# Sums over channels as products of split operands, and norm 1's row factors transposed later

## The chip, the cores and the metric

The kernel runs on one core of a Trainium2 chip. The core has a matrix engine (TensorE, PE in the profile), a vector engine (DVE), an activation engine (ACT), a general engine (POOL), and DMA queues that SyncE (SP) and POOL issue. Each engine works through its own instructions in order and waits on semaphores for the others. The metric is the time of one execution on the device in microseconds, as a median over runs. Three runs of the kernel before took 1290.13, 1290.21 and 1290.51 us, median 1290.21.

## The reference, cut to what matters

The kernel computes one layer of a sequence model in float32: 1024 tokens, 1024 channels. Two token mixers run on the same normalised input and are merged by gates; then comes a squared-ReLU MLP. There are four RMS norms, each with a mean over the channels of a token.

```python
def rmsnorm(x, gain):
    xf = x.astype(jnp.float32)
    y = xf * lax.rsqrt(jnp.mean(xf * xf, axis=-1, keepdims=True) + RMS_EPS)
    return (y * gain.astype(jnp.float32)).astype(x.dtype)
...
        h = rmsnorm(x, g_pre_mix)                       # norm 1
        proj = jnp.einsum('bsd,de->bse', h, w_in)       # [u_pool | q | k | v]
...
        mix = jnp.einsum('bsd,de->bse', merged, w_out)
        x = x + rmsnorm(mix, g_post_mix)                # norm 2
        h2 = rmsnorm(x, g_pre_mlp)                      # norm 3
        a = jnp.square(jax.nn.relu(jnp.einsum('bsd,df->bsf', h2, w_up)))
        ff = jnp.einsum('bsf,fd->bsd', a, w_down)
        x = x + rmsnorm(ff, g_post_mlp)                 # norm 4
```

The numbers of the norms in the comments are those used below.

## The kernel before

Channels lie on the 128 partitions and tokens along the free axis, in two halves of 512 tokens (h = 0 and 1). A dense layer is a chain of 128x512 products into one PSUM bank. Each operand is split into two parts of the reduced float type fp32r (hi, and lo = value - hi), and mm3 (L104 to L114) makes three products of each step: hi by hi (L112), hi by lo (L113), lo by hi (L114). Weights come by DMA into wraw; ACT casts them to whi (L82), which has three buffers, and DVE makes the remainder wlo (L83).

A norm needs the mean over channels, which lie on partitions. ACT squares the tiles, DVE adds them into acc, and one product with a 128x128 matrix of 1/1024 (ones) leaves the mean ms of every token on all partitions. That product is a plain float32 one. rstd (L145 to L158) then makes the row factor rb: ACT takes a logarithm and an exponential (L153 or L151, and L154), and DVE polishes the result in three steps (L155, L156, L157).

- Norm 1 is in phase_in, in stats(h) (L330 to L340), which is interleaved with the products of the first projection u for the second half (stats_side, L353). Since the gain is already in hT, rb is only applied where a projection leaves PSUM (u_out, L380; job_qk, L464). For v, which has tokens on partitions, rb is needed as a column: four PE transposes (L336) into a tile rt, and a DVE copy of one column of each block into rcol (L337).
- In phase_in the tiles ms and rt of both halves, and the tile dm of pool_mix's first half, share one PSUM buffer (tag "o"). Each has to wait until the one before it has been read.
- u has four groups of channels. Groups 0 to 2 of both halves come first, into banks of two kinds (du and zu); group 3 follows in the loop behind u_out(1), and takes the banks du of group 0 over once DVE's L380 has read them. pool_group and pool_mix make the pooling mixer on DVE, ACT and PE beside it. After the loop come the q and k projections (job_qk, tile dqk), and v (job_v, tile dv, read by L497 with rcol).
- Norms 2 and 3 are in chain(ch, h, mix, acc) (L826, L846), which runs beside other products. Norm 3's result is split by ACT (hi) and DVE (t_lo, L812); with it start the MLP's products, which work on pairs of weights and their sums (L911, L912).
- Norm 4 is norm() inside down() (L1200, L1201). There the last squares are not added to acc: two products, one of acc and one of the last squares, are summed in PSUM. The second half's runs beside the products of p3, and the first half's in two parts of 256 tokens at the end.

The order of the instructions on each engine is not written by hand: a scheduler sets it when the program is built, from the order of the code, the buffers and modelled durations.

Of the kernel before, what the change touches and what calls it, by code (L numbers as in the profile page):

```python
# [19 lines left out]
F32 = mybir.dt.float32  # L20
F32R = mybir.dt.float32r
BF16 = mybir.dt.bfloat16
AF = mybir.ActivationFunctionType
ALU = mybir.AluOpType
# [5 lines left out]
P = 128  # L30
H = 512
# [18 lines left out]
class Block:  # L50
# [106 lines left out]
        nc.vector.scalar_tensor_tensor(out=y, in0=b, scalar=-3.0, in1=y, op0=ALU.add, op1=ALU.mult)  # L157
        return y  # L158

    def split_gain(self, src, gain, r, hi, lo, pool):  # L160

        nc = self.nc
        n = src.shape[-1]
        f = pool.tile([P, H], F32, name="nf", tag="nf", bufs=4)[:, :n]
        nc.vector.scalar_tensor_tensor(out=f, in0=src, scalar=gain, in1=r, op0=ALU.mult, op1=ALU.mult)
        nc.scalar.copy(hi, f)
        nc.vector.tensor_sub(lo, f, hi.bitcast(F32))

    def build(self):
        tc, nc = self.tc, self.nc  # L170
        self.table_inst = None
        order = [(("u", g), O_U + g) for g in (0, 1, 2, 3)]
        order += [(("q", 0), O_QK), (("k", 0), O_QK + 1)]
        self.fill = {
# [10 lines left out]
        }  # L185
        order += [(("v", 0, j), O_V + j) for j in range(2)]
        for h in range(-1, 9):
            for f in self.fill[h]:
                if f[0] == "v":
                    if f[1] == 0:  # L190
                        order += [(("v", 1, j), O_V + 2 + j) for j in range(2)]
                elif f[0] == "g":
                    if f[-1] != 1 or len(f) == 2:
                        order.append((f[:2], O_G + f[1]))
                else:
                    order.append((f, O_QK + 2 * f[1] + (f[0] == "k")))
        order += [(("br", e), O_BR + e) for e in range(8)]
        kept = {3: "t2_hi", 4: "t2_lo"}
        order += [(("out", 0, e), O_OUT + e, (), None, kept.get(e)) for e in range(8)]
        order += [(("out", 1, e), O_OUT + e) for e in (2, 1, 0)]  # L200
        order += [(("up", i), O_UP + self.pair(i)[0]) for i in range(16)]
        self.set_order(order)

        cp = tc.alloc_tile_pool(name="const", bufs=1, side="left")
        self.wp = tc.alloc_tile_pool(name="weights", bufs=1, side="left")
        self.big = tc.alloc_tile_pool(name="big", bufs=1, side="left")
        dp = tc.alloc_tile_pool(name="scratch", bufs=1, space=DRAM)
        self.gscr = [dp.tile([P, 1024], F32, name=f"gscr{i}") for i in range(16)]
        self.yscr = [[dp.tile([P, 1024], F32R, name=f"yscr{i}_{j}") for j in range(2)] for i in range(4)]
        self.pscr = [[dp.tile([P, 4, H], F32, name=f"pscr{i}_{j}") for i in range(4)] for j in range(2)]  # L210
        self.ascr = [[dp.tile([P, 4, H], F32, name=f"ascr{f}_{h}") for h in range(2)] for f in range(8)]
        self.tscr = [dp.tile([P, 4, H], F32, name=f"tscr{f}") for f in range(4)]
        self.wscr = [[dp.tile([P, 4, 512], F32, name=f"wscr{n}_{q}") for q in range(4)] for n in range(4)]
        self.wsums = self.weight_sums()
        self.xscr = [[dp.tile([P, H], F32, name=f"xscr{h}_{e}") for e in range(8)] for h in range(2)]

        self.vt = cp.tile([P, N_VEC], F32, name="vt")
        nc.scalar.preload_act_table_set(TABLES)
        self.ones = cp.tile([P, P], F32, name="ones")
        nc.vector.memset(self.ones, 1.0 / 1024.0)  # L220
        self.one1 = cp.tile([P, 1], F32, name="one1")
        nc.vector.memset(self.one1, 1.0)
        self.eps = cp.tile([P, 1], F32, name="eps")
        nc.vector.memset(self.eps, EPS)
        self.gn = cp.tile([P, 32], F32, name="gn")
        self.eye = cp.tile([P, P], F32, name="eye")

        self.past = cp.tile([P, 1024], mybir.dt.uint8, name="past")
        self.rcnt = cp.tile([P, 16], F32, name="rcnt")

        self.rp = tc.alloc_tile_pool(name="row", bufs=1, side="left")
        self.rb = [self.rp.tile([P, H], F32, name=f"rb{h}") for h in range(2)]
        self.rcol = cp.tile([P, NK], F32, name="rcol")
        edge = tc.alloc_tile_pool(name="edge", bufs=1, side="right")
        self.edge = edge.tile([P, 24], F32, name="edge")
        self.dps = tc.alloc_tile_pool(name="att_d", bufs=2, space=PSUM)
        self.zps = tc.alloc_tile_pool(name="att_z", bufs=1, space=PSUM)
        self.phase_in()
        self.phase_attention()
        self.phase_post()  # L240
        self.phase_mlp()

        edge.release()
        for p in (self.rp, self.big, self.wp, cp, dp):
            p.release()


    def phase_in(self):
        tc, nc = self.tc, self.nc
        pa = tc.alloc_tile_pool(name="in_a", bufs=1, side="right")  # L250
        xs = [pa.tile([P, NK, H], F32, name=f"x{h}") for h in range(2)]

        def load(h, k, n):
            nc.sync.dma_start(xs[h][:, k : k + n, :], self.x[h][:, k : k + n, :])
# [3 lines left out]
        for g in range(3):  # L258
            pool, tag, n = (self.wp, "wraw", 2) if g < 2 else (pa, "uraw", 1)
# [33 lines left out]
        for t, src in zip((self.eye, self.rcnt), self.consts):  # L293
# [4 lines left out]
            out=past, in_=past, pattern=[[1, 1024]], compare_op=ALU.is_ge, fill=0.0, base=P - 1024,  # L298
# [11 lines left out]
        accs = []  # L310
        for h in range(2):
            hi = self.big.tile([P, NK, H], F32R, name=f"hT_hi{h}", tag=f"big_hi{h}")
            lo = self.big.tile([P, NK, H], F32R, name=f"hT_lo{h}", tag=f"big_lo{h}")
            self.hT.append((hi, lo))
            acc = pa.tile([P, H], F32, name="acc", bufs=2)
            accs.append(acc)
            for k in range(NK):
# [3 lines left out]
                    out=lo[:, k, :], in0=xs[h][:, k, :], scalar=g, in1=hi[:, k, :].bitcast(F32),  # L321
# [8 lines left out]
        def stats(h):  # L330
            ms = self.zps.tile([P, H], F32, name="ms", tag="o", bufs=1)
            nc.tensor.matmul(ms, self.ones, accs[h], start=True, stop=True)
            self.rstd(ms, pa, ("sq", 3), out=self.rb[h])
            rt = self.zps.tile([P, H], F32, name="rt", tag="o", bufs=1)
            for j in range(4):
                nc.tensor.transpose(rt[:, j * P : j * P + P], self.rb[h][:, j * P : j * P + P], self.eye)  # L336
            nc.vector.tensor_copy(  # L337
                self.rcol[:, 4 * h : 4 * h + 4].rearrange("p (j o) -> p j o", o=1),
                rt.rearrange("p (j o) -> p j o", o=P)[:, :, 0:1],
            )  # L340
# [35 lines left out]
        def u_out(g, ps):  # L376
            if g not in us:
                us[g] = self.op.tile([P, 1024], F32, name=f"u{g}", tag=f"oT{g}")
            for h, d in ps:
                nc.vector.tensor_mul(us[g][:, h * H : h * H + H], d, self.rb[h])  # L380
# [47 lines left out]
        for h in range(2):  # L428
            d = self.dps.tile([P, H], F32, name="du", tag="d")
            self.dense(d, self.weights(("u", 3)), self.hT[h])  # L430
            u_out(3, [(h, d)])
            if h == 0:
                pool_mix(0, pooled[0])
                pooled.append(pool_group(1))
                u_out(2, list(enumerate(dst[2])))
        self.run(self.job_qk("q", 0, 0))
        pool_mix(1, pooled[1])
        pooled.append(pool_group(2))
# [375 lines left out]
    def chain(self, ch, h, mix, acc):  # L814
# [8 lines left out]
        tmp = self.hp.tile([P, 4, H], F32, name=f"tmp{h}", tag="t3_hi")  # L823
        yield 3
        ms = self.ps.tile([P, H], F32, name="ms", tag="ms", bufs=1)
        nc.tensor.matmul(ms, self.ones, acc, start=True, stop=True)  # L826
        r = self.rstd(ms, ch, None, bufs=1, b=tmp[:, 3, :])
        acc2 = ch.tile([P, H], F32, name="acc2", bufs=1)
        for e in range(8):
# [13 lines left out]
                nc.vector.tensor_add(acc2, acc2, sq)  # L843
        yield 28
        ms = self.ps.tile([P, H], F32, name="ms", tag="ms", bufs=1)
        nc.tensor.matmul(ms, self.ones, acc2, start=True, stop=True)  # L846
        self.rstd(ms, ch, None, out=self.rb[h], b=tmp[:, 3, :])

        def norm(e):
# [192 lines left out]
    def down(self):  # L1042
# [152 lines left out]
        def norm(h, x1, gap, c=slice(0, H), behind=(None,)):  # L1195
# [1 line left out]
            at = gap  # L1197
            yield at
            ms = self.ps.tile([P, H], F32, name="ms", tag="ms", bufs=1)[:, c]
            nc.tensor.matmul(ms, self.ones, accs[h][:, c], start=True, stop=False)  # L1200
            nc.tensor.matmul(ms, self.ones, last[h], start=False, stop=True)  # L1201
            r = self.rb[h][:, c]
            self.rstd(ms, mp, ("r", 4), n=c.stop - c.start, out=r)
            nxt = None if x1 else residual(h, 0)
# [121 lines left out]
```

## Time and profile before

| what | value |
|---|---|
| median of three runs | 1290.21 us |
| profiled execution, its own time | 1291.31 us |
| span in its trace | 1289.5 us |
| mean granted TensorE clock | 0.994 |
| q1, the larger DMA queue, share of 16 engines | 33.8% |
| HBM read and written | 178.10 MB, 83.89 MB |

The page begins with the busy time of each engine, and then shows the span in 40 slices of 32 us; a digit is the busy share of a slice in tenths. PE is the matrix engine, PEld its weight loads, which run beside it. PEclk is the clock that the throttle granted. The kinds of product that take most time are the three of mm3; each group of the page is a line of the code with one form of tiles. Rows in order of time give the start, the duration, the engine, the line, the operation, output and inputs; in brackets stands how long the engine was idle before, and for what it waited. An f32 product is recorded as two matmuls (x2).

### The profile page before, as it was taken

What the parts mean: (1) busy time and instruction counts of PE and PEld (TensorE: products, weight loads), DVE (VectorE), ACT (ScalarE), POOL (GpSimd) and SP (SyncE); (2) the same over time, 40 slices, a digit from 0 to 9 for tenths busy, and PEclk for the clock granted to TensorE, in tenths of its full rate; (3) what the DMA queues carried; (4) which work ended last, traced back from release to release, by engine and by line L of the source; (5) the groups of instructions that cost most, each with busy time, mean ns of one, the idle gap of its engine ahead of it and who ended that gap; (6) DMA issues with size and microseconds to landing.
All of it is one profiled execution on the core that took longest, in us unless ns stands there. A gap on an engine that the chain in (4) does not pass through costs nothing.

```text
span 1289.5 us, 16851 instructions
## 1 busy us (share of the span) xinstructions
PE 1268.3 (98%) x6145; PEld 1063.1 (82%) x6145; DVE 924.2 (72%) x1303; ACT 605.5 (47%) x989; POOL 175.2 (14%) x346
## 2 busy tenths in 40 slices
PE   9899999999999999999999999999999999999996
PEld 6688888998888888888877888888888888888885
DVE  8686587688777756661667979777775655776876
ACT  8145455555555543232446646545554433344341
POOL 1011213202322331000101002211220000001000
PEclk9899999999999999999999999999999999999998
DMA  6152646624837978451338577756569546547641
GB/s 223 50 176 81 225 123 164 131 67 113 214 123 177 296 204 234 158 180 49 136 109 285 184 249 254 244 190 210 190 226 342 186 157 225 190 173 246 239 160 66
DMA packets 75746, 233.72 MB, mean 181 GB/s; under 512 B 8624, under 2 KB 11184, under 8 KB 73488
## 3 DMA queue, kind: packets, MB, share of 16 engines
q1 hardware_dynamic: 47936, 143.64, 33.8%
q0 software_dynamic: 27152, 88.49, 23.1%
q8 instruction: 48, 0.79, 0.3%
q10 hardware_dynamic: 576, 0.52, 0.1%
q14 instruction: 34, 0.28, 0.1%
HBM read 178.10 MB, written 83.89 MB: 203 GB/s over the span
## 4 chain that ended last, share of the span: by engine, by line
PE 88%; DVE 6%; DMA 2%; issue 2%; ACT 1%; SPq 0%; POOL 0%; DVEq 0%; POOLq 0%; ACTq 0%
PE d L114 18%; PE d L112 18%; PE d L113 18%; PE dg L110 5%; PE dg L114 5%; PE dg L113 5%; PE o L606 3%; PE at L581 2%; PE dqk L113 2%; PE dqk L114 2%; PE dqk L110 2%; DMA wraw<-w 2%; PE z L552 1%; PE z L549 1%; DVE wlo L83 1%
## 5 line engine op out<-in xcount | busy, mean ns | idle before, releaser
L113 PE MATMUL d<-blo,whi 128*128 128x512 f32 (+1 forms) x456 | 172.7, 379 | 0.0
L114 PE MATMUL d<-bhi,wlo 128*128 128x512 f32 (+1 forms) x456 | 171.9, 378 | 0.0
L112 PE MATMUL d<-bhi,whi 128*128 128x512 f32 (+1 forms) x456 | 168.4, 378 | 0.0
L562 DVE TENSOR_TENSOR_SCAN F<-F,past 128x384 f32<-128x384 f32 (+3 forms) x96 | 93.5, 974 | 25.8 <-ACT F L553 24.9
L82 ACT CAST whi<-wraw 128x512 fp32r<-128x512 f32 (+1 forms) x88 | 67.7, 799 | 88.5 <-PE d L113 33.9
L110 PE MATMUL dg<-hT_hi,whi 128*128 128x512 f32 x256 | 103.3, 404 | 0.3 <-DVE v L497 0.3
L83 DVE TENSOR_TENSOR wlo<-wraw,whi 128x512 fp32r<-128x512 f32 (+1 forms) x88 | 78.2, 907 | 34.1 <-ACT whi L82 34.1
L113 PE MATMUL dg<-hT_lo,whi 128*128 128x512 f32 x256 | 100.6, 393 | 0.0
L114 PE MATMUL dg<-hT_hi,wlo 128*128 128x512 f32 x256 | 100.4, 392 | 0.0
L113 PEld LDWEIGHTS d<-blo,whi 128*128 128x128 f32 x456 | 85.7, 188 | 16.3 <-issue 0.2
L114 PEld LDWEIGHTS d<-bhi,wlo 128*128 128x128 f32 x456 | 85.8, 188 | 16.0 <-issue 0.2
L112 PEld LDWEIGHTS d<-bhi,whi 128*128 128x128 f32 x456 | 85.5, 188 | 15.9
L553 ACT ACTIVATE F<-z 128x384 f32<-128x384 f32 (+3 forms) x96 | 47.3, 493 | 64.1 <-DVE T L566 38.4
L113 PE MATMUL d<-b_lo,whi 128*128 128x512 f32 x196 | 76.7, 391 | 0.0
L112 PE MATMUL d<-b_hi,whi 128*128 128x512 f32 x196 | 75.6, 390 | 0.0
L114 PE MATMUL d<-b_hi,wlo 128*128 128x512 f32 x196 | 75.3, 392 | 0.1
L1093 DVE TENSOR_TENSOR wlo<-slots_hi,whi 128x1024 fp32r<-128x1024 f32 x29 | 35.5, 1224 | 52.6 <-ACT whi L1091 52.5
L1091 ACT CAST whi<-slots_hi 128x1024 fp32r<-128x1024 f32 x29 | 30.5, 1051 | 84.5 <-PE d L113 64.9
L589 DVE TENSOR_TENSOR alo<-at,ahi 128x512 fp32r<-128x512 f32 (+1 forms) x80 | 50.6, 633 | 26.6 <-ACT ahi L588 25.9
L1091 ACT CAST whi<-slots_lo 128x1024 fp32r<-128x1024 f32 x27 | 28.4, 1052 | 72.9 <-PE d L113 59.2
L566 DVE TENSOR_TENSOR T<-T,F 128x127 f32<-128x127 f32 (+4 forms) x96 | 53.1, 556 | 10.2 <-POOL T L556 4.2
L1093 DVE TENSOR_TENSOR wlo<-slots_lo,whi 128x1024 fp32r<-128x1024 f32 x27 | 33.0, 1222 | 36.7 <-ACT whi L1091 36.7
(305 smaller groups left out, 3335.2 us busy)
## 6 DMA issues: line engine op xcount, KB each, us to landing
wraw<-w SPq DMA_DIRECT2D x80, 512.0 KB, 4.3
wscr<-w POOLq DMA_DIRECT2D x24, 1024.0 KB, 9.4
ext_b<-ascr SPq DMA_DIRECT2D x40, 512.0 KB, 4.4
gscr<-gs POOLq DMA_DIRECT2D x32, 256.0 KB, 4.6
gate<-gscr POOLq DMA_DIRECT2D x16, 512.0 KB, 3.7
pscr<-p SPq DMA_DIRECT2D x32, 256.0 KB, 3.7
braw<-w SPq DMA_DIRECT2D x16, 512.0 KB, 5.4
ascr<-c POOLq DMA_DIRECT2D x32, 256.0 KB, 5.2
```

The source lines that it names most:

```text
L82: nc.scalar.copy(hi[:, c], raw[:, c])
L83: self.last_lo = nc.vector.tensor_sub(lo[:, c], raw[:, c], hi[:, c].bitcast(F32)).ins
L110: nc.tensor.matmul(ps, wh, rh, start=first and i == 0, stop=False)
L112: nc.tensor.matmul(ps, wh, rh, start=first and i == 0, stop=False)
L113: nc.tensor.matmul(ps, wh, rl, start=False, stop=False)
L114: nc.tensor.matmul(ps, wl, rh, start=False, stop=last and i == n - 1)
L553: nc.scalar.activation(f[:, c : c + n], z[:, :n], AF.Sigmoid, scale=-1.0)
L562: nc.vector.tensor_tensor_scan(fr, fr, past[:, c : c + n][:, ::-1], 1.0 if top else f[:, c + n : c + n + 1], ALU.mult, ALU.max)
L566: nc.vector.tensor_mul(tl[:, c:e], tl[:, c:e], f[:, c + 1 : e + 1])
L589: nc.vector.tensor_sub(lo[:, c0:], at[:, c0:], hi[:, c0:].bitcast(F32))
L1091: last_split[0] = nc.scalar.copy(hi, src).ins
L1093: last_split[1] = nc.vector.tensor_sub(lo, src, hi.bitcast(F32)).ins
```

## The change

The diff, cut to its core:

```diff
-    def split_gain(self, src, gain, r, hi, lo, pool):
...
+    def channel_sum(self, ps, acc, pool, tag, bufs):
+
+        nc = self.nc
+        hi, lo = (pool.tile([P, H], F32R, name=f"acc_{n}", tag=tag, bufs=bufs) for n in ("hi", "lo"))
+        nc.scalar.copy(hi, acc)
+        nc.vector.tensor_sub(lo, acc, hi.bitcast(F32))
+        nc.tensor.matmul(ps, self.ones_r, hi, start=True, stop=False)
+        nc.tensor.matmul(ps, self.ones_r, lo, start=False, stop=True)
...
-        self.ones = cp.tile([P, P], F32, name="ones")
-        nc.vector.memset(self.ones, 1.0 / 1024.0)
-        self.one1 = cp.tile([P, 1], F32, name="one1")
-        nc.vector.memset(self.one1, 1.0)
+        self.ones_r = cp.tile([P, P], F32R, name="ones")
+        self.ones = self.ones_r.bitcast(F32)
...
+        mean = pa.tile([P, P], F32, name="mean")
+        nc.vector.memset(mean, 1.0 / 1024.0)
+        nc.vector.tensor_copy(self.ones_r, mean)
...
             ms = self.zps.tile([P, H], F32, name="ms", tag="o", bufs=1)
             nc.tensor.matmul(ms, self.ones, accs[h], start=True, stop=True)
             self.rstd(ms, pa, ("sq", 3), out=self.rb[h])
+
+        def columns(h):
+
             rt = self.zps.tile([P, H], F32, name="rt", tag="o", bufs=1)
             for j in range(4):
                 nc.tensor.transpose(rt[:, j * P : j * P + P], self.rb[h][:, j * P : j * P + P], self.eye)
...
                 u_out(2, list(enumerate(dst[2])))
+        for h in range(2):
+            columns(h)
         self.run(self.job_qk("q", 0, 0))
...
-        nc.tensor.matmul(ms, self.ones, acc, start=True, stop=True)
+        if h == 0:
+            nc.tensor.matmul(ms, self.ones, acc, start=True, stop=True)
+        else:
+            self.channel_sum(ms, acc, ch, "nf", 2)
...
-        nc.tensor.matmul(ms, self.ones, acc2, start=True, stop=True)
+        if h == 0:
+            nc.tensor.matmul(ms, self.ones, acc2, start=True, stop=True)
+        else:
+            self.channel_sum(ms, acc2, ch, "nf", 2)
...
-            nc.tensor.matmul(ms, self.ones, accs[h][:, c], start=True, stop=False)
-            nc.tensor.matmul(ms, self.ones, last[h], start=False, stop=True)
+            if h == 0:
+                nc.tensor.matmul(ms, self.ones, accs[h][:, c], start=True, stop=False)
+                nc.tensor.matmul(ms, self.ones, last[h], start=False, stop=True)
+            else:
+                nc.vector.tensor_add(accs[h], accs[h], last[h])
+                self.channel_sum(ms, accs[h], mp, "r", 4)
```

There are two parts. For the second half of the tokens, norms 2, 3 and 4 sum over channels with two fp32r products, of the hi and the lo part of the sum of squares, in place of one f32 product (two in norm 4, where a DVE addition now joins the last squares to the sum first). ACT and DVE make the two parts. The matrix of means becomes an fp32r tile, filled by a memset and a DVE copy. Norm 1, and all norms of the first half, keep their f32 products. The second part moves the transposes of norm 1 out of stats(h): those of both halves now stand behind the loop over u's last group, ahead of the q projections. split_gain and one1 had no use.

The scheduler's order changes with it. On PE, towards the end of the first three groups of u, before (-) and now (+); zu is a bank of the projection, and the number 290 or 291 marks the second half's operand:

```order
 L112 MATMUL zu<-hT_hi_290,whi 128x512
 L113 MATMUL zu<-hT_lo_291,whi 128x512
-L114 MATMUL zu<-hT_hi_290,wlo 128x512
-L112 MATMUL zu<-hT_hi_290,whi 128x512
-L113 MATMUL zu<-hT_lo_291,whi 128x512
-L114 MATMUL zu<-hT_hi_290,wlo 128x512
-L112 MATMUL zu<-hT_hi_290,whi 128x512
-L113 MATMUL zu<-hT_lo_291,whi 128x512
-L336 MATMUL rt<-eye,rb_165 128x128 x4
+L333 MATMUL ms<-acc,ones 128x512
```

The transposes of the first half (rt) stood here, and the second half's sum (ms, now L333) stands six products ahead of their place. Before, that sum came 20 products after the transposes. A few us later on PE, where group 3 of u begins (du, operand 249):

```order
 L112 MATMUL zu<-hT_hi_290,whi 128x512
-L332 MATMUL ms<-acc,ones 128x512
 L113 MATMUL zu<-hT_lo_291,whi 128x512
 L114 MATMUL zu<-hT_hi_290,wlo 128x512
-L336 MATMUL rt<-eye,rb_166 128x128 x4
+L112 MATMUL zu<-hT_hi_290,whi 128x512
+L113 MATMUL zu<-hT_lo_291,whi 128x512
+L114 MATMUL zu<-hT_hi_290,wlo 128x512
+L112 MATMUL zu<-hT_hi_290,whi 128x512
+L113 MATMUL zu<-hT_lo_291,whi 128x512
+L114 MATMUL zu<-hT_hi_290,wlo 128x512
 L112 MATMUL du<-hT_hi_249,whi 128x512
```

Before, the second sum, two products and the second transposes came directly ahead of du; now only products do, and 28 of them stand between the second sum and du. The two moved sets of transposes now stand among the products of the q projection: the first of them 25 products after the last product of pool_mix(0), the second 29 products later. On ACT the cast of the weights for q's projection now stands between the logarithm and the exponential of norm 1's second half; the cast that stood there before is the next one.

On DVE and ACT, norm 3 of the second half changes as well. DVE before, from the last squares added to the start of the normalised tiles (mix):

```order
L843 TENSOR_TENSOR acc_6277<-acc_6277,tmp_6246 128x512 x6
L83 TENSOR_TENSOR wlo<-wraw,whi 128x1024 x2
L155 SCALAR_TENSOR_TENSOR tmp_6246<-ms,rb_166 128x512
L156 TENSOR_TENSOR tmp_6246<-tmp_6246,rb_166 128x512
L83 TENSOR_TENSOR wlo<-wraw,whi 128x1024
L157 SCALAR_TENSOR_TENSOR rb_166<-tmp_6246,rb_166 128x512
L851 SCALAR_TENSOR_TENSOR mix_0_5908<-mix_0_5908,gn,rb_166 128x512
```

And DVE in the changed kernel at the same place:

```order
L852 TENSOR_TENSOR acc_6282<-acc_6282,tmp_6246 128x512 x6
L83 TENSOR_TENSOR wlo<-wraw,whi 128x1024
L165 TENSOR_TENSOR acc_lo<-acc_6282,acc_hi 128x512
L83 TENSOR_TENSOR wlo<-wraw,whi 128x1024 x2
L155 SCALAR_TENSOR_TENSOR tmp_6246<-ms,rb_163 128x512
L156 TENSOR_TENSOR tmp_6246<-tmp_6246,rb_163 128x512
L157 SCALAR_TENSOR_TENSOR rb_163<-tmp_6246,rb_163 128x512
L863 SCALAR_TENSOR_TENSOR mix_0_5908<-mix_0_5908,gn,rb_163 128x512
```

The new subtraction (L165) stands between the weight splits, and all three splits now come ahead of the norm's own three steps, where one of them came after the second step before. On ACT the logarithm was followed directly by the exponential; now a weight cast and the copy of a finished product (p) stand between the two. Further on, before the MLP's first products, four subtractions t_lo followed the last weight split (L83); now five do, since one that stood ahead of it comes behind it. In norm 4 of the second half the sum's product of hi comes 24 products later than the f32 sums did, and that of lo nine or ten after it. Elsewhere the order on PE is nearly the same.

More of the change, by code (lines that the diff above doesn't have):

```diff
@@ L158, in rstd @@
         return y
-    def split_gain(self, src, gain, r, hi, lo, pool):
+    def channel_sum(self, ps, acc, pool, tag, bufs):
         nc = self.nc
[L163 to L167, printed above, removed]
+        hi, lo = (pool.tile([P, H], F32R, name=f"acc_{n}", tag=tag, bufs=bufs) for n in ("hi", "lo"))
[3 more added lines that the diff above has]
+        nc.tensor.matmul(ps, self.ones_r, lo, start=False, stop=True)
     def build(self):
```

## The prediction

> **What bounds the kernel now.** I read the shares of busy time first, then what TensorE (PE) waited for, then the one long wait in order of time, and last the granted clock around it.
>
> ```profile
> span 1289.5 us, 16851 instructions
> PE 1268.3 (98%) x6145; PEld 1063.1 (82%) x6145; DVE 924.2 (72%) x1303; ACT 605.5 (47%) x989; POOL 175.2 (14%) x346
> PEclk9899999999999999999999999999999999999998
> ...
> PE rt L336 <- DVE rb L157: 4.6, 1, 4.6
> PE dv L112 <- DVE v L497: 0.4, 1, 0.4
> PE dg L110 <- DVE v L497: 0.3, 1, 0.3
> ```
>
> PE is busy for 98% of the span. What can be saved is therefore PE work, PE waits, or clock. One wait stands out in the list of waits (total, times, longest, in us): the transposes of norm 1's second row factor waited 4.6 us for DVE. The clock row dips once after the start, in the second slice (32 to 64 us), which is where this wait lies. The rows around it, in order of time (start, duration, engine, what waited for what):
>
> ```profile
> 41.40 1.02 PE L332 MATMUL ms<-acc,ones 128*128 128x512 f32 x2
> 41.86 0.80 PE L113 MATMUL zu<-hT_lo,whi 128*128 128x512 f32 x1
> 42.46 0.69 ACT L153 ACTIVATE rb<-ms,eps 128x512 f32<-128x512 f32 x1 [5.52 <-PE ms L332]
> 42.50 0.40 PE L114 MATMUL zu<-hT_hi,wlo 128*128 128x512 f32 x1
> 43.05 1.03 ACT L82 CAST whi<-wraw 128x1024 fp32r<-128x1024 f32 x1
> 46.70 0.69 DVE L157 SCALAR_TENSOR_TENSOR rb<-nb,rb 128x512 f32<-128x512 f32 x1
> 47.31 1.28 DVE L380 TENSOR_TENSOR u<-du,rb 128x512 f32<-128x512 f32 x2
> 47.45 1.11 PE L336 MATMUL rt<-eye,rb 128*128 128x128 f32 x4 [4.55 <-DVE rb L157]
> 48.21 0.77 PE L112 MATMUL du<-hT_hi,whi 128*128 128x512 f32 x1
> ...
> 61.30 0.39 PE L112 MATMUL dqk<-hT_hi,whi 128*128 128x512 f32 x1
> ```
>
> PE runs the sum over channels (ms), two more products, and then stands from 42.90 to 47.45 while ACT and DVE turn ms into rb. The clock falls in this wait:
>
> ```profile
> 41.00:48.00 7.00, 2.45 (x10) 1.44 (x9) 3.82 (x6) 2.15 (x3) 0.00 (x0) 0.84 0.25 71
> 48.00:53.00 5.00, 5.00 (x15) 3.98 (x14) 5.00 (x10) 0.00 (x0) 0.00 (x0) 0.54 0.06 23
> 53.00:61.00 8.00, 8.00 (x37) 6.59 (x36) 7.21 (x13) 1.05 (x1) 0.00 (x0) 1.00 0.01 2
> 966.00:1190.00 224.00, 224.00 (x990) 185.54 (x989) 141.82 (x138) 91.76 (x99) 6.40 (x12) 1.00 0.62 216
> ```
>
> The columns are stretch, length, busy time and count of PE, weight loads, DVE, ACT and POOL, then the clock. A mean of 0.84 over 7 us is 2.2 us at half clock, so it fell at about 45.8, and 0.54 over the next 5 us puts its return at about 52.6. The last row gives the price of one 128x512 product at full clock: 224.00 / 990 = 0.226 us. (The matmul durations of single rows overlap, so starts are what I subtract.)
>
> **The change, part by part.** The profiled execution took 1291.31 us, 1.10 above the median of 1290.21. I sum against the former and carry the result to the latter.
>
> *1. The second ms comes earlier.* The order of PE's instructions now has ms (second half) where the first half's transposes stood, less six products; 28 products follow it and then du. In the old order it had to wait its turn for the one PSUM buffer that ms and rt share.
>
> ```profile
> 30.37 0.68 DVE L328 TENSOR_TENSOR acc<-acc,sq 128x512 f32<-128x512 f32 x1
> 35.90 1.05 ACT L82 CAST whi<-wraw 128x1024 fp32r<-128x1024 f32 x1 [3.70 <-PE zu L113]
> 36.38 0.60 PE L336 MATMUL rt<-eye,rb 128*128 128x128 f32 x4
> 36.73 0.48 PE L114 MATMUL zu<-hT_hi,wlo 128*128 128x512 f32 x1
> ```
>
> The old first transposes started at 36.38; six products earlier is 36.38 - 6 x 0.226 = 35.02. The sum's input acc is complete at 31.05, so nothing holds it there. An f32 sum costs 42.50 - 41.40 - 0.23 = 0.87 us. With 28 products behind it, PE reaches du at 35.02 + 0.87 + 28 x 0.226 = 42.22 instead of 48.21: **-5.99 us**. This counts the idle time and both sets of transposes as gone from here.
>
> Is the wait then gone, or does du inherit it? The same DVE chain that releases rt also frees du's PSUM bank: du needs the first of the two L380 multiplies, which ended at about 47.95, 0.26 before du started. So moving the transposes alone would gain next to nothing; the earlier ms is what pays. On ACT a weight cast stands between the two steps of the norm, at 35.90 before, released by PE. It comes 0.87 later now, behind ms: 36.77. From such a cast to the end of the first L380 the old chain took 47.95 - 43.05 = 4.90. That frees the bank at 41.7, and PE arrives at 42.22. The margin is 0.5 us. If one more cast of 1.05 stood ahead, du would wait 0.5; zero is my value, 0.5 the bad end.
>
> *2. The clock stays up.* From 48.21 to 61.30 PE ran 48 products of du in 13.09 us. At 0.226 they take 10.85: **-2.24 us**. Without a PE wait of several us there is no row in this stretch that would lower the clock. If it fell nonetheless, 0.
>
> On the timed runs, as against the profiled one, a page speaks against counting this. The Trainium skill ("TensorE: Matmul & The Clock Gate", section "What's actually happening") says that the clock halves after at least one idle window of about 3.4 us, and that the window is free-running. An estimate from that page: a wait of 4.55 us holds a whole window in (4.55 - 3.4) / 3.4 = 1/3 of the phases only, so the median run would not have lost the clock and could not regain it. The trace shows a fall after 2.9 us of idle time, which that window as stated would not give.
>
> *3. The transposes are paid later.* Four cost 36.73 - 36.38 = 0.35 us at full clock, and two sets now stand between the q projections: **+0.70**. The end to the bad side is 48.21 - 47.45 = 0.76 a set at half clock, +1.52.
>
> *4. What follows, up to the attention.* PE arrives 8.23 - 0.70 = 7.5 us earlier there. DVE's own chain starts from the first L380, which moves by 47.95 - 41.7 = 6.2. If DVE were the limit, PE would give back 7.5 - 6.2 = 1.3. If PE stays the limit, and v's multiply (L497) is in time, the two waits of 0.4 and 0.3 go. I take **-0.4**, near the latter, since DVE follows PE through much of this stretch (it sat 3.40 us before the row at 66.99 below). Ends: -0.7 and +1.3.
>
> *5. Norms 2 and 3, second half.* Each f32 sum of 0.87 becomes two products of 0.45: -0.42 each. The new ACT copy and DVE subtraction stand ahead of the sum. In norm 2 DVE has 6.06 us of idle time soon after, which hides them:
>
> ```profile
> 677.05 1.23 DVE L83 TENSOR_TENSOR wlo<-wraw,whi 128x1024 fp32r<-128x1024 f32 x1 [6.06 <-ACT whi L82]
> ...
> 705.02 0.63 ACT L154 ACTIVATE rb<-rb 128x512 f32<-128x512 f32 x1
> 706.90 1.05 ACT L82 CAST whi<-wraw 128x1024 fp32r<-128x1024 f32 x1 [1.25 <-DMA wraw<-w]
> 707.85 0.58 ACT L959 COPY p<-d 128x512 f32<-128x512 f32 x1
> 709.12 0.69 DVE L157 SCALAR_TENSOR_TENSOR rb<-tmp,rb 128x512 f32<-128x512 f32 x1
> 740.09 2.51 DVE L812 TENSOR_TENSOR t_lo<-mix,t_hi 128x512 fp32r<-128x512 f32 x4
> 750.11 0.40 PE L113 MATMUL d<-b_lo,whi 128*128 128x512 f32 x1
> 750.57 0.50 PE L114 MATMUL d<-t_hi,wlo 128*128 128x512 f32 x1
> ```
>
> Norm 3 is less lucky. In the new order the norm's second ACT step (the exponential, at 705.02 before) stands behind the cast at 706.90 and the copy at 707.85, and DVE's three steps behind one more weight split. The exponential then ends at 708.43 + 0.63 = 709.06, and three DVE steps of 0.69 with small gaps end at about 711.25 instead of 709.81: 1.45 late. DVE then works through the normalised tiles up to 742.6 and makes the first pair's weight remainders, for which PE already waits 0.23 (750.11 to 750.57 is 0.46): no slack. One more t_lo subtraction (at 740.09, four take 2.51, or 0.6 each) now comes behind the last weight split instead of ahead of it, which takes 0.6 of the lateness off the path. So 1.45 - 0.6 = 0.85 is late there, norm 3's own 0.42 is lost in that wait, and norm 2's is kept: 0.85 - 0.42 = **+0.43**. Ends: -0.84 if nothing is late, 1.45 + 0.58 (one more copy ahead) - 0.42 = +1.6.
>
> *6. Norm 4, second half.*
>
> ```profile
> 1196.83 1.02 PE L1200 MATMUL ms<-acc,ones 128*128 128x512 f32 x2
> 1197.68 1.02 PE L1201 MATMUL ms<-sq,ones 128*128 128x512 f32 x2
> 1198.77 0.40 PE L114 MATMUL d<-bhi,wlo 128*128 128x512 f32 x1
> ```
>
> Two f32 sums with one product among them take 1198.77 - 1196.83 = 1.94, so 1.71 without it. Two split products take 0.45: **-1.26**. The extra DVE addition of 0.69 and the split are hidden by later work: 80 us of products follow, and DVE is busy only 141.82 of 224 us here.
>
> *7. Start.* One DVE cast in place of a memset, before the first product is possible: 0.
>
> Sum: -5.99 - 2.24 + 0.70 - 0.40 + 0.43 - 1.26 = -8.76. 1291.31 - 8.76 = 1282.55, and 1.10 less on the median: **1281.5 us**.
>
> **The rivals.**
>
> *DVE becomes the limit (0.16).* The bad ends above at once or in part: +1.7 at the attention, +1.2 at the pair, +0.5 at du, +0.8 for slow transposes. For it speaks that DVE is the engine waited for in every row of the list above; against it the slack before 66.99. Time: 1283.4 to 1285.8.
>
> *The clock gives nothing back on the median (0.08).* Either du still waits long enough, or the timed runs had full clock. The sum is short by term 2: 1281.5 + 2.24 = 1283.7. The three timed runs of before lie within 0.38 us, less than 2.24, so all of them had the fall or none had. The free-running window of the Trainium skill's clock page would give this time; that the runs agree so closely speaks against its chance phase.
>
> *The wait moves from rt to du (0.09).* If the bank of du came free only at its old 47.95, terms 1, 2 and 4 shrink to 0.26 in all: 1290.21 - 0.26 + 0.70 + 0.43 - 1.26 = 1289.8. That is the case in which the change does not do what its order promises. For it: du hangs on the same chain. Against: every step of that chain is released by ms or by a cast that PE releases early.
>
> *The wait comes back at the moved transposes, and the kernel is slower (0.06).* The first moved set needs the shared buffer, which pool_mix(0) holds until its L419 has read dm:
>
> ```profile
> 66.29 0.39 PE L114 MATMUL dm<-ph,wml 128*128 128x512 f32 x1
> 66.99 1.41 DVE L419 SCALAR_TENSOR_TENSOR u<-dm,vt,win 128x512 fp32r<-128x512 f32 x2 [3.40 <-ACT win L418]
> ```
>
> Before, L419 ended 68.40 - 66.68 = 1.7 us after the last dm product. In the new order 25 products (5.7 us) stand between, so PE has 4.0 us in hand; the weight split (1.23) and q steps (3 x 0.69) now ahead of L419 on DVE could take 3.3 of it. If DVE were later than that by W, PE would stand for W and, from about 3 us on, lose the clock's 2.24 again. The gain is used up at W = 8.76 - 2.24 = 6.5 us. At W = 10 it is 1281.5 + 10 + 2.24 = 1293.7. For it: PE comes 8 us earlier to work that DVE has only 6 us earlier. Against: 6.5 us more is far beyond any DVE queue seen here.
>
> **How the numbers follow.** The forecast (1279.6 to 1283.4, with the good ends of terms 4 and 5: -0.3 and -1.27) gets 0.58, something better 0.03, the rivals 0.16, 0.08, 0.09 and 0.06 in the order above. The range 1279.6 to 1285.8 holds forecast and the first two rivals, 0.82. A measurement here can tell about 0.2% (2.6 us) from no change, so faster means under 1287.6: 0.58 + 0.03 + 0.16 + 0.08 = 0.85. Within: 0.09. Slower: 0.06.
>
> **What would show it.** Right: no PE wait before du, granted clock 1.00 between 41 and 61 us, du starting near 42.2, split sums that take about 0.45, a wait of about 1 us at the first pair's remainder near 742 (750 less 8). Wrong: an idle PE before du, rt or dv; a clock below 1 before 70 us; or a wait at the first pair longer than 2.5 us. If the clock row dips in both kernels, term 2 was no gain.

## The result and the profile after

The changed kernel takes 1296.35 us (six runs, 1296.05 to 1296.80), the kernel before 1290.36 (six runs, 1289.94 to 1292.05): a ratio of 1.0045, with a 95% interval of 1.0032 to 1.0058. It is slower by 6 us, where 1281.5 was forecast and 1285.8 was the upper end of the range. The profiled execution has a span of 1294.5 us. Among the comparisons below, one of the four executions of e3 took 3300.68 us and is left out of its ratio; the only trace kept of e3 is of that execution, with every fp32r product of 128x512 at about 619 ns for a reason that is not known, so e3 is read by its times alone.

From the page of the changed kernel, the span, the busy shares, the clock row and the shares of the chain that ended last; then its list of PE's waits (total, times, longest):

```profile
span 1294.5 us, 16855 instructions
PE 1278.2 (99%) x6143; PEld 1060.0 (82%) x6143; DVE 927.5 (72%) x1307; ACT 609.5 (47%) x992; POOL 175.4 (14%) x346
PEclk9999999999999999999999999999999999999998
PE 98%; DVE 1%; DMA 0%; ACT 0%; SPq 0%; issue 0%; DVEq 0%
...
PE idle L308 <- DVE zero L305: 1.4, 1, 1.4
PE d L112 <- DVE oT L619: 0.9, 1, 0.9
PE ms L1213 <- DVE acc L1253: 0.8, 1, 0.8
```

All that the forecast wanted to see at norm 1 is there: the wait of rt has gone, those of dv and dg too, and the clock row has no dip. Yet PE is busy for 1278.2 us instead of 1268.3, with two recorded matmuls fewer. So the time did not go into a wait. PE does the same work for longer, at full clock. The same stretches as before (length, busy time and count of PE, weight loads, DVE, ACT, POOL, then clock, DMA share, GB/s) show where:

```profile
41.00:48.00 7.00, 7.00 (x33) 5.79 (x32) 7.00 (x12) 1.06 (x1) 0.00 (x0) 1.00 0.11 43
48.00:53.00 5.00, 5.00 (x24) 4.14 (x23) 5.00 (x9) 1.19 (x2) 0.00 (x0) 1.00 0.28 107
966.00:1190.00 224.00, 224.00 (x962) 180.03 (x962) 136.12 (x131) 86.42 (x91) 5.67 (x12) 1.00 0.60 208
```

In the last stretch PE is busy throughout and the clock is 1.00 in both kernels, but it does 962 products in 224 us where it did 990: 0.233 us each instead of 0.226. PE's own rows of the changed kernel in order of time show the step from one to the other inside the MLP:

```profile
801.16 0.39 PE L114 MATMUL d<-t_hi,slo 128*128 128x512 f32 x1
801.39 0.39 PE L112 MATMUL d<-t_hi,shi 128*128 128x512 f32 x1
801.62 0.39 PE L113 MATMUL d<-t_lo,shi 128*128 128x512 f32 x1
801.84 0.40 PE L114 MATMUL d<-t_hi,slo 128*128 128x512 f32 x1
802.08 0.39 PE L112 MATMUL d<-t_hi,whi 128*128 128x512 f32 x1
802.31 0.40 PE L113 MATMUL d<-t_lo,whi 128*128 128x512 f32 x1
802.55 0.39 PE L114 MATMUL d<-t_hi,wlo 128*128 128x512 f32 x1
```

The moving operand (t_hi, t_lo, the two parts of norm 3's result) comes from the same side of memory throughout. While the weights are shi and slo (the two parts of a sum of weights), starts lie 0.22 to 0.23 apart; from the product ahead of the first whi on, 0.23 to 0.24. What sets shi apart from whi is where the tiles lie. Start addresses in bytes per partition, as the built programs list them:

```
tile                   side    before   after
one1                   left     17248   (gone)
eps                    left     17280    17248
whi, first buffer      left     27264    27232
hT_hi, b_hi of h = 0   left     51840    51808
shi, first buffer      right   155520   155520
```

The diff also deletes one1, a tile of 4 bytes that nothing read. Tiles are placed in steps of 32 bytes (one1 and eps, of 4 bytes each, lie 32 apart), so everything behind it on the left side moved down by 32. Tiles on the right side stayed. Before, every operand of an fp32r product started at the same remainder modulo 256 (27264, 51840 and 155520 all leave 128). Afterwards left tiles leave 96 and right tiles 128. The 128x512 products of the changed kernel's trace, sorted by the remainders of their moving operand and of the next product's weights, which load beside it:

```
moving  next weights  products  median spacing (ns)
  96        96          2117         227
  96       128           365         235
 128        96          2048         234
 128       128           256         230
(kernel before: all 4778 at 128 and 128, median 227)
```

Equal remainders keep 227 ns. (In the last group 181 products lie in the MLP, with a median of 227; 59 lie in the attention, at 230. The attention's products with k as moving operand had 230 before the change too.) Unequal ones cost 234 or 235. This is theory A of the experiments, first held with a unit of 64 bytes: a product is slower where its moving operand and the weights differ in phase, that is, in the remainder of their start addresses. Rival B is that the change's work slows the products, rival C that a tile at certain addresses is slow by itself. 2413 pairs at 233.3 - 226.7 = 6.6 ns (the means in stretches of the MLP) are 15.9 us, close to the 14.9 by which the forecast was missed.

### The profile page after: what moved, and what is told of

Same layout as the page of the kernel before. It is cut to its first block, busy times and chain, and to the rows that moved or that the text cites. A ratio compares the mean times of both kernels' runs of the same rounds, so it can differ in the third digit from the quotient of the medians.

```text
span 1294.5 us, 16855 instructions
## 1 busy us (share of the span) xinstructions
PE 1278.2 (99%) x6143; PEld 1060.0 (82%) x6143; DVE 927.5 (72%) x1307; ACT 609.5 (47%) x992; POOL 175.4 (14%) x346
## 4 chain that ended last, share of the span: by engine, by line
PE 98%; DVE 1%; DMA 0%; ACT 0%; SPq 0%; issue 0%; DVEq 0%
PE d L113 20%; PE d L114 20%; PE d L112 20%; PE dg L114 5%; PE dg L110 5%; PE dg L113 5%; PE o L612 3%; PE at L587 2%; PE dqk L114 2%; PE dqk L113 2%; PE dqk L110 2%; PE z L558 1%; PE z L555 1%; PE dv L114 1%; PE dv L113 1%; PE dv L112 1%
## 5 line engine op out<-in xcount | busy, mean ns | idle before, releaser
L83 DVE TENSOR_TENSOR wlo<-wraw,whi 128x512 fp32r<-128x512 f32 (+1 forms) x88 | 78.2, 907 | 30.8 <-ACT whi L82 30.8
```

The source lines that it names most:

```text
L83: self.last_lo = nc.vector.tensor_sub(lo[:, c], raw[:, c], hi[:, c].bitcast(F32)).ins
```

## The experiments

**One: the address alone (e1 to e4).** Each runs the same instructions in the same order on every engine as the kernel it starts from; only places differ.

e1, the changed kernel with 32 bytes put back:

```diff
-        self.eps = cp.tile([P, 1], F32, name="eps")
+        self.eps = cp.tile([P, 9], F32, name="eps")[:, :1]
```

> The changed kernel with 32 bytes per partition put back ahead of all other tiles of the left side of SBUF (a wider eps tile; nothing reads the new columns). Every engine runs the same instructions in the same order. Theory A (a product is 6.5 ns slower where the start addresses of its moving operand and of the next product's weights differ by 32 bytes modulo 64; 2413 of the changed kernel's 128x512 products do, and none did before): the 15.7 us are gone, 1281 to 1283 us, pitch 227 ns throughout the MLP. Rival B (the new splits, sums or the moved transposes slow the products): unchanged, 1296. Rival C (a tile that is off a multiple of 64 is slow by itself): as A, 1281 to 1283.

Measured: 1280.56 us, ratio to before 0.9924 (0.9910 to 0.9939). The changed kernel is 15.8 us faster for a slot of 32 bytes that nobody reads, and it is now faster than both kernels.

e2, the kernel before with its left side moved down:

```diff
-        self.one1 = cp.tile([P, 1], F32, name="one1")
-        nc.vector.memset(self.one1, 1.0)
-        self.eps = cp.tile([P, 1], F32, name="eps")
+        pair = cp.tile([P, 2], F32, name="one1")
+        nc.vector.memset(pair[:, :1], 1.0)
+        self.eps = pair[:, 1:2]
```

> The kernel before with one1 and eps in one tile, so that the left side moves down by 32 bytes as in the changed kernel; the same instructions in the same order. Theory A: 2404 products at 6.5 ns more are 15.6 us, so 1304 to 1306 us, with the 4.6 us wait of rt still there and a pitch of 233 ns in most of the MLP. Rival B: 1290, as before. Rival C: as A, 1304 to 1306.

Measured: 1306.52 us, ratio 1.0125 (1.0110 to 1.0140): 16.1 us more. The shift costs the same with nothing else of the change present, so rival B is out. The stretch 966 to 1190 us, first of e1 and then of e2:

```profile
966.00:1190.00 224.00, 224.00 (x990) 185.49 (x989) 145.67 (x143) 91.39 (x98) 4.27 (x8) 1.00 0.62 216
```

```profile
966.00:1190.00 224.00, 224.00 (x963) 180.10 (x962) 135.20 (x131) 88.83 (x95) 4.83 (x9) 1.00 0.58 203
```

990 products against 963 in the same time: e1 has the spacing of the kernel before, e2 that of the changed one.

e3, the changed kernel with the right side moved down as well:

```diff
-        self.edge = edge.tile([P, 24], F32, name="edge")
+        self.edge = edge.tile([P, 32], F32, name="edge")[:, :24]
```

> The changed kernel, its left side where the change puts it (32 modulo 64), with the right side moved by 32 bytes as well (a wider edge tile). All operands of products then start at 32 modulo 64, but none differs from its neighbour. Same instructions, same order. Theory A: 1281 to 1283 us, pitch 227. Rival B: 1296. Rival C (each tile off a multiple of 64 is slow): all 4700 products pay, some 1311 us.

Measured: 1280.26 us, ratio 0.9922 (0.9905 to 0.9938). No operand starts at a multiple of 64 here, and the loss is gone all the same. Rival C is out: it is the difference between the two operands that counts.

e4, the changed kernel with its left side moved up by 64:

```diff
-        self.eps = cp.tile([P, 1], F32, name="eps")
+        self.eps = cp.tile([P, 17], F32, name="eps")[:, :1]
```

> The changed kernel with the left side moved by 64 bytes from where the change puts it, so that it is at 32 modulo 64 again, one slot higher than before the change. Same instructions, same order. Theory A: the phase is again apart by 32, so 1296 us as the changed kernel. Were it the place as such, or one conflict of two certain tiles, rather than the phase modulo 64: another time, near 1282. Rival B: 1296.

Measured: 1296.87 us, ratio 1.0052 (1.0035 to 1.0068). Another place with the same difference, and the same loss.

**Two: the period (e8, e9, e10).** e8 puts the left side of the changed kernel 64 bytes above its place in the kernel before:

```diff
-        self.eps = cp.tile([P, 1], F32, name="eps")
+        self.eps = cp.tile([P, 25], F32, name="eps")[:, :1]
```

> The changed kernel with the left side 64 bytes above its place in the kernel before. Phase modulo 64 as there, modulo 128 not. Theory A with 64 bytes as the unit: as e1_left_back_by_32, 1280 to 1281 us. If the unit is 128 bytes: 1296, as the changed kernel, or more.

Measured: 1296.34 us, ratio 1.0049 (1.0035 to 1.0063). My unit of 64 bytes was wrong: a difference of 64 costs as much as 32. e9, the same with 128 bytes:

```diff
-        self.eps = cp.tile([P, 1], F32, name="eps")
+        self.eps = cp.tile([P, 41], F32, name="eps")[:, :1]
```

> The changed kernel with the left side 128 bytes above its place in the kernel before; same instructions, same order. In the kernel before, operands whose phases differ by 256 bytes run at 227 ns, and e8_left_up_64 showed 64 to be as slow as 32. Theory A with a period of 128 bytes: as e1_left_back_by_32, 1280 to 1281 us. With a period of 256 bytes: 1296.

Measured: 1296.21 us, ratio 1.0040 (1.0026 to 1.0055). So 128 isn't the period either. In the kernel before, 365 pairs of remainder 128 and 384 modulo 512 keep a median of 227, so 256 is the first period that fits.

e10 measures the cost by itself. Its core (a moving operand shifted by m bytes, weights by w, over eight PSUM banks):

```diff
+        def stretch(steps):
+            nonlocal n
+            for i in range(64):
+                m, w = steps[i % len(steps)]
+                a, c = 64 + m // 4 + 512 * (i % 2), 64 + w // 4 + 128 * (i % 8)
+                nc.tensor.matmul(banks[n % 8], wt[:, c : c + P], mov[:, a : a + H], start=True, stop=True)
+                n += 1
```

> A kernel of 24 stretches of 64 fp32r products of 128x512, with no other engine at work; it computes nothing of the layer, and only the spacing of its products is read. Stretches 1 to 14 move the start of the moving operand by 0, 0, 4, 8, 16, 32, 48, 64, 96, 128, 160, 192, 224 and 256 bytes against fixed weights; 15 to 19 move the weights by 4, 16, 32, 64, 128; 20 moves both by 32; 21 to 24 alternate between two phases, so that the moving operand agrees with its own weights (21, 23) or with the next product's weights (22, 24). Theory A: 227 ns at 0 and 256, about 233 at 32, 64, 96, whichever operand moves; 227 where both move; and where they alternate, 233 if own and next weights both count, 227 in 21 and 23 if the own weights decide, 227 in 22 and 24 if the next do. At 4, 8 and 16 bytes open: 227 if the unit is 32 bytes, 233 if any shift counts. Rival (the slower spacing needs the traffic of the other engines): 227 everywhere.

Two groups of its page, all of PE's work and one of the two casts that are all of DVE's:

```profile
L74 PE MATMUL bank<-mov,wt 128*128 128x512 f32 x1536 | 358.0, 395 | 7.8 <-DVE mov L65 7.8
...
L65 DVE CAST mov<-raw 128x2048 fp32r<-128x2048 f32 x1 | 1.2, 1219 | 0.0
```

Mean of 54 spacings in the middle of each stretch, in ns, from the starts in the trace (the first of the two stretches at 0, whose first products lie about 0.4 us apart, is left out):

```
moving by   0     4     8     16    32    48    64    96    128   160   192   224   256
          226.7 236.7 231.6 231.7 233.4 233.3 228.9 233.3 233.3 234.3 233.3 233.3 226.7
weights by        4           16    32          64          128
                232.4       233.3 233.3       233.3       232.5
both by 32                                                226.7
alternating, own weights agree and the next differ by 32  233.3
alternating, next weights agree and own differ by 32      231.6
alternating by 64, own agree / next agree                 231.6 / 231.7
```

The traffic of other engines isn't needed. Every difference tried that isn't a multiple of 256 bytes costs 2 to 10 ns in 227, a shift by one element too. It costs whichever operand moves, though not the same: moving by 4 is the dearest at 236.7, weights by 4 have 232.4. Where the phases alternate, both orders are slow: a product's moving operand has to agree with its own weights and with the next ones. The trace of the changed kernel says the same: 147 of its products agree with their own weights and not with the next, at a median of 235, and 20 the other way round, at 233.

**Three: the parts of the change, on the old layout (e5, e6, e7).** e5 is the kernel before with the transposes split off from stats(h) and called after the loop, as in the change; one1 stays.

```diff
             self.rstd(ms, pa, ("sq", 3), out=self.rb[h])
+        def columns(h):
             rt = self.zps.tile([P, H], F32, name="rt", tag="o", bufs=1)
...
+        for h in range(2):
+            columns(h)
         self.run(self.job_qk("q", 0, 0))
```

> The kernel before with the transposes moved and nothing else (sums stay f32; one1 stays, so all tiles stay where they were). By terms 1 to 4 of the prediction: -5.99 - 2.24 + 0.70 - 0.40 = -7.9, so 1282 to 1283 us, no wait of PE before du, full clock from 41 to 61 us. Rival (du inherits the wait): 1289 to 1290, with a PE wait before du that ends with L380.

Measured: 1282.67 us, ratio 0.9944 (0.9931 to 0.9956): -7.6 us against 1290.29. There is no wait before du. In its trace du starts at:

```profile
42.00 0.39 PE L112 MATMUL du<-hT_hi,whi 128*128 128x512 f32 x1
```

42.22 was worked out. e6 is e1 with the transposes put back into stats(h), so that only the split sums are new.

```diff
-        def columns(h):
...
-        for h in range(2):
-            columns(h)
```

> The split sums of norms 2, 3 and 4 with norm 1's transposes left in stats(h), and the left side of SBUF where it was before the change. By terms 5 and 6: +0.43 - 1.26 = -0.8, so 1289 to 1290 us, with the 4.6 us wait of rt still there and a small wait at the first pair of the MLP. If the products' lower cost counted in full (-0.84 - 1.26): 1288.3. If the added work on ACT and DVE cost more than the products save: over 1290.5.

Measured: 1288.25 us, ratio 0.9985 (0.9976 to 0.9994): -2.0 us, more than the -0.8 expected and at the good end of term 5; its interval, -3.1 to -0.8, just reaches the expected value.

e7 is e1 with norm 3's second half back on its f32 product.

```diff
-            self.channel_sum(ms, acc2, ch, "nf", 2)
+            nc.tensor.matmul(ms, self.ones, acc2, start=True, stop=True)
```

> The changed kernel with the left side put back by 32 bytes, and norm 3 of the second half with its f32 product again. By term 5 the split of norm 3 cost 0.85 of lateness and saved 0.42 that was lost in the wait: 0.4 us less than e1_left_back_by_32, so 1280.1 us, and no wait of d L113 for b_lo at the first pair. Rival (the split was free there): 0.4 us more than that kernel, 1281.0.

Measured: 1284.31 us, ratio 0.9949 (0.9937 to 0.9962), 3.75 us slower than e1. It doesn't isolate norm 3. With that edit the scheduler also put the work of the first MLP pairs in another order on DVE, ACT and SP. PE's waits in it:

```profile
PE d L114 <- DVE slo L924: 1.1, 2, 0.9
...
PE d L112 <- DVE u L1012: 0.6, 1, 0.6
PE d L113 <- DVE b_lo L818: 0.4, 1, 0.4
```

The wait for b_lo, which I had put down to norm 3's lateness, stays at 0.4 us: it lies at 656 us, ahead of norm 2's sum and 39 us before norm 3's. 0.7 more at slo and 0.6 at u are new. The f32 sum accounts for another 0.4. The remaining 2 us are not explained; 0.7 of them lie, in the profiled executions, ahead of that wait (655.83 us against 655.09 in e1).

## Why the prediction was wrong

**The step that failed** is term 7, "One DVE cast in place of a memset, before the first product is possible: 0", together with what I put into it. The diff's deletions, one1 among them, I counted as instructions only. That the deleted tile moves every left tile by 32 bytes had no term at all, and no rival covered it: all of mine were waits or the clock. It cost 15.8 us (after to e1; 16.1 from before to e2), more than the whole gain. The other side of the same fault is the price of "one 128x512 product at full clock: 224.00 / 990 = 0.226 us", which I carried to the new kernel as if it were a constant. It holds only while the operands' phases agree.

The rest can be read off e1, e5 and e6, where the layout is as before:

- *Terms 1 to 4* (-7.93 in all): right in sum. e5 gave -7.6. In the changed kernel's trace, the rows of the steps that were worked out:

```profile
34.76 1.02 PE L333 MATMUL ms<-acc,ones 128*128 128x512 f32 x2
36.52 1.05 ACT L82 CAST whi<-wraw 128x1024 fp32r<-128x1024 f32 x1
40.80 1.28 DVE L384 TENSOR_TENSOR u<-du,rb 128x512 f32<-128x512 f32 x2
42.01 0.39 PE L112 MATMUL du<-hT_hi,whi 128*128 128x512 f32 x1
67.25 0.60 PE L340 MATMUL rt<-eye,rb 128*128 128x128 f32 x4
```

ms starts at 34.76 (35.02 worked out), the cast at 36.52 (36.77), the first L384 ends at about 41.4 (41.7), du starts at 42.01 (42.22). All of these are about 0.25 early because PE is: the same product starts at 14.58 us instead of 14.84. The margin before du is the half microsecond that was stated. The moved transposes have no wait in the list, and the waits of dv and dg are gone.

- *Term 2* depends on the execution. e2 has the same wait for rt, but its clock in the two stretches reads:

```profile
41.00:48.00 7.00, 2.45 (x11) 1.49 (x9) 4.09 (x6) 2.15 (x3) 0.00 (x0) 0.93 0.27 74
48.00:53.00 5.00, 5.00 (x19) 4.04 (x18) 5.00 (x10) 0.00 (x0) 0.00 (x0) 0.75 0.01 3
```

That is 1.0 and 2.5 us at half clock, 3.5 together, against 2.2 and 4.6 (6.8) in the profiled execution of before. So the wait cost less clock there. Half-clock stretches of 3.5 and 6.8 us, one and two steps of about 3.4 us, agree with the free-running window in the Trainium skill ("TensorE: Matmul & The Clock Gate", "What's actually happening"); and the three executions profiled with this wait (before, e2, e6) all lost some clock. e5's -7.6 lies nearer to the sum with this term (-7.9) than to that without (-5.7), but its interval (-8.9 to -5.7) reaches to both. The granted clocks on record speak for the term: the fifteen executions of before in that comparison have a mean of 0.9945, e5's five one of 0.9966. Over some 1289 us that is 2.7 us of full clock, where the term took 2.24.

- *Term 5* (+0.43): wrong sign by the rows of e1, small. Norm 3 and the first pair there:

```profile
694.70 0.39 PE L166 MATMUL ms<-acc_hi,ones 128*128 128x512 f32 x1
696.86 1.04 ACT L82 CAST whi<-wraw 128x1024 fp32r<-128x1024 f32 x1
700.52 0.69 DVE L157 SCALAR_TENSOR_TENSOR rb<-tmp,rb 128x512 f32<-128x512 f32 x1
735.30 0.69 DVE L932 TENSOR_TENSOR sums<-wraw 128x512 f32<-128x512 f32 x1 [1.31 <-DMA wraw<-w]
740.95 0.47 PE L114 MATMUL d<-t_hi,wlo 128*128 128x512 f32 x1
741.26 0.40 PE L112 MATMUL d<-t_hi,whi 128*128 128x512 f32 x1
```

I had the cast wait for its weights as late as before. Here it follows the logarithm at once, 2.16 us after the sum began instead of 3.66, and L157 ends 6.51 us after the sum's start instead of 6.57. Nothing was late: DVE still waits 1.31 us for weights ahead of the pair, and PE's spacing there is 0.31, so it waits 0.08. The step that failed here is "no slack": in the kernel before, DVE already waited for weights at the same place, longer than the lateness that was worked out:

```profile
744.95 0.69 DVE L920 TENSOR_TENSOR sums<-wraw 128x512 f32<-128x512 f32 x1 [2.35 <-DMA wraw<-w]
```

With both savings of 0.42 and norm 4's 1.26, the sum would be -2.1; e6 gave -2.0. One cost had no term: ahead of norm 2's sum, PE now waits for the first half's b_lo, which the list of waits of the kernel before does not have, and this takes most of norm 2's saving back. The row in e1:

```profile
655.09 0.50 PE L113 MATMUL d<-b_lo,whi 128*128 128x512 f32 x1 [0.38 <-DVE b_lo L818]
```

- *Sum.* Without the shift the forecast of 1281.5 stands against 1280.56 (e1) and 1280.26 (e3). With it, 1280.56 + 15.9 = 1296.5 against 1296.35. Two ends of the range do not follow from their terms: 1281.5 - 0.3 - 1.27 is 1279.9 and not 1279.6, and 1281.5 with the four bad ends of 1.7, 1.2, 0.5 and 0.8 is 1285.7 and not 1285.8. Neither matters beside 15 us.
- *Rivals.* None of the four happened. The slower one had the right sign for a reason that did not occur: PE doesn't wait at the moved transposes.

## What to carry to other kernels

A diff that removes, adds or resizes a tile, however small, can move all tiles allocated behind it on its side: compare the start addresses of the operands of hot products before and after, modulo 256 bytes between moving operand and weights. If busy time on TensorE grows while waits and clock are fine, divide a busy stretch by its count of products in both kernels; a spacing that steps with the name of a tile points to its place. For fp32r products of 512 columns, make the pools on both sides of memory start at equal remainders, with a few padding bytes; it was worth 1.2% here.

## What the runs showed of the hardware

A 128x512 fp32r product took 226.7 ns where moving operand and weights started at the same address modulo 256 bytes, and 229 to 237 where they did not, with nothing else running (e10). The common offset itself does not matter (e3; both by 32 in e10). 128x256 products showed no such cost: in the changed kernel 204 with unlike phases between moving operand and next weights had a median of 118 ns, 712 with like phases 120. The Trainium skill ("TensorE: Matmul & The Clock Gate", "Step-by-step: what each phase is for") says that loading the next tile's weights doesn't steal read bandwidth from the running product, since the two have their own ports. For fp32r products of 512 columns e10 shows a limit of this: the two are not independent, since the spacing depends on how their start addresses relate (226.7 against 228.9 to 236.7 ns). What conflicts inside the chip was not measured.
